# One fp32 transformer layer on one core: gate rows by two fp32r products, a reordered lead-in, and sixteen loads from GpSimd that nobody reads

## The chip, the core and the metric

The kernel runs on one NeuronCore of a Trainium2 chip. The core has five engines with an in-order instruction queue each: TensorE (PE, matrix products into PSUM), VectorE (DVE), ScalarE (ACT), GpSimd (POOL) and SyncE (SP, which here only issues transfers). Sixteen DMA engines move data between HBM and the on-chip memory (SBUF). The metric is the device time of one execution in microseconds, lower is better.

## The reference

The layer takes 256 latent tokens and 256 context tokens of width 2048, with fp32 weights:

```
sh1, sc1, g1, sh2, sc2, g2 = split(silu(c) @ w_ada + b_ada, 6)          # c is one row; 2048 -> 6 x 2048
x = layer_norm(alpha * x + g1 * (attention(x, ctx) @ w_out), ln1)       # modulated inputs, w_in, 16 heads
u = x * (1 + sc2) + sh2
x = layer_norm(alpha * x + g2 * ((silu(u @ w_gate) * (u @ w_up)) @ w_down), ln2)
```

`w_gate` and `w_up` are 2048 x 5632, `w_down` is 5632 x 2048. Only `g2`, the gate of the last residual, matters to the arithmetic of the change: it is a row of 2048 numbers, needed on all 128 partitions.

## The kernel before, in words

**Products.** Each fp32 weight piece is split into a high and a low part in fp32r: ACT copies the raw piece to `hi` (a cast), DVE subtracts (`lo = raw - hi`), and three PE products hi x hi, lo x hi and hi x lo replace one fp32 product (`mm3`, L292 to L294). Raw pieces of 1 MB (four tiles of 128 x 512) land in a ring of four buffers `raw`; split halves (128 x 1024) live in a ring of four slots `hi`/`lo`. A raw buffer is free for the next load when DVE has made its second `lo`.

**The lead-in** (first 25 us). A planner (`Flow`) orders the steps of the whole first phase with estimated times; some steps are then "pulled" to a place by hand (`F.pulls`: a trigger step, and the steps emitted right behind it). At the start two 1 MB pieces of `w_ada` come in four quarters each, PE multiplies them by silu(c) as they land (`flow_columns`, function `quarters`, L595), and the result modulates the first 128 columns of x and ctx: an ACT step and a DVE step `modulate`, then the low part `rest`. The first piece of `w_in` is split meanwhile (steps `w0`, `l0`: cast and low part), then pieces 1, 2 and 3 (`lead["w", i]`). Fillers (`warm`, L342) are small products of a constant, issued in gaps of PE. `evacs` are the copies of finished sums out of PSUM: rows 0 and 2 on ACT (L778), rows 1 and 3 on DVE (L782).

**The last stage** (from about 878 us). `w_down` is applied in four column blocks of 512 (n = 0 to 3), each in eleven steps of four tiles (`step`, 24 PE products for the 256 tokens), which I call steps 0 to 10. Beside it the gate row `g2` is made, 512 columns at a time (`gate2_steps`): GpSimd clears `adav` (L393), SP loads 512 numbers of `b_ada` into its first partition (L399), four loads of 1 MB of `w_ada` follow (L406), and DVE accumulates each of their sixteen tiles, scaled by silu(c), into `adav` (L416). One PE product with a 128 x 128 matrix of ones in plain fp32 (`rows_from`, L426) sums over the partitions and puts the row on all of them, and ACT copies it to `g2sb` (L427). There are four such rows; rows 0 and 1 are made during n = 0, rows 2 and 3 during n = 1 and n = 2. There is one buffer `adav`, so GpSimd may clear it for the next row only when the last row's product has read it.

In this stage the tile framework decides the order on each engine from simulated times; SP issues `w_down`, `w_ada` and `b_ada` loads from one queue, in that order, and a load that waits for its buffer or its semaphore holds all loads behind it.

Of the kernel before, what the change touches and what calls it, by code (L numbers as in the profile page):

```python
# [12 lines left out]
F32 = mybir.dt.float32  # L13
F32R = mybir.dt.float32r
# [4 lines left out]
ALU = mybir.AluOpType  # L19
# [3 lines left out]
P = 128  # L23
D = 2048
# [11 lines left out]
NB = 512  # L36
G4 = 4
SUB = 2
# [179 lines left out]
def dit_layer(ctx: ExitStack, tc: tile.TileContext, x, c, cx, c_ctx, w_ada, b_ada, w_in, q_norm_g,  # L218
              k_norm_g, sink_logit, w_out, ln1_g, ln1_b, w_gate, w_up, w_down, ln2_g, ln2_b,
              rope_cos, rope_sin, out):  # L220
    nc = tc.nc
    x, c, cx = x[0], c, cx[0]
    w_ada, w_in, w_out, w_gate, w_up, w_down = (w[0] for w in (w_ada, w_in, w_out, w_gate, w_up, w_down))
# [3 lines left out]
    whl = ctx.enter_context(tc.tile_pool(name="whl", bufs=HL_BUFS))  # L227
# [3 lines left out]
    def acc_bank():  # L231
        return acc_ps.tile([P, NB], F32, tag="acc", name="acc")

    def wk_bank():
        return wk_ps.tile([P, NB], F32, tag="wk", name="wk")

    def run(steps):
        for s in steps:
            s()

    def merge(*lists):

        keyed = [((i + 0.5) / len(l), n, i, s) for n, l in enumerate(lists) for i, s in enumerate(l)]
        return [e[3] for e in sorted(keyed, key=lambda e: e[:3])]
# [42 lines left out]
    def split(hi, lo, src):  # L287
        nc.scalar.copy(hi, src)
        nc.vector.tensor_tensor(lo, src, hi.bitcast(F32), op=ALU.subtract)
# [50 lines left out]
    def warm(wps, n):  # L340
        for _ in range(n):
            nc.tensor.matmul(wps, lhsT=ident, rhs=ident, start=True, stop=True)  # L342

    wps = Buf("wk")
# [16 lines left out]
    ones = main.tile([P, P], F32, tag="ones", name="ones")  # L361
# [10 lines left out]
    def ada_vector_steps(starts, width, sums, done):  # L372


        st = {}
        ns = len(starts)
        w = ns * width
        nk = G4 * NB // w

        def step(g):  # L380
            if g == 0:
                st["a"] = first_sums(sums(), starts, width)
            raw = raw_tile()
            vector_load(raw, starts, width, g)
            for i in range(G4 * NB // min(w, 2 * NB)):
                vector_sum(raw, st["a"], w, g, i)
            if g == KD // nk - 1:
                done(st["a"])

        return [lambda g=g: step(g) for g in range(KD // nk)]  # L390
# [29 lines left out]
    def vector_sums(width):  # L420
        return main.tile([P, 2 * NB], F32, tag="adav", name="adav")[:, :width]

    def rows_from(sb, dst, s):

        ps = wk_bank()
        nc.tensor.matmul(ps, lhsT=ones, rhs=sb[:, s : s + NB], start=True, stop=True)  # L426
        return lambda: nc.scalar.copy(dst[:, s : s + NB], ps)  # L427

    def ada_rows(c0, dst, sums):
        def done(sb):  # L430
            for s in range(0, dst.shape[-1], NB):
                rows_from(sb, dst, s)()

        return ada_vector_steps((c0,), dst.shape[-1], sums, done)

# [24 lines left out]
    def const_tables():  # L460
        nc.gpsimd.tensor_scalar_mul(nsink, sinkb, -1.0)
        for t in range(NT):
            for g, cg, sg in ((gq, cosQ, sinQ), (gk, cosK, sinK)):
# [18 lines left out]
    F = Flow({"raw": RAW_BUFS, "araw": ADA_BUFS, "hl": HL_BUFS, "acc": 4, "wk": 4, "b4": NB4, "t2k": T2K},  # L482
             {"SP": 2100.0, "PE": 3800.0, "ACT": 4300.0, "DVE": 4000.0, "POOL": 4000.0})
# [6 lines left out]
    def t2k(name, shape=(P, NB), dtype=F32):  # L490
        return pa.tile(list(shape), dtype, tag="t2k", name=name, bufs=T2K)
# [87 lines left out]
    last_load, lead = [], {}  # L579

    def flow_columns(c0, ncol, shift, scale, ats, at):

        width = ncol * P
        n1 = ncol == 1
        nk = G4 * NB // width
        ns = KD // nk
        bank, prev = Buf("wk"), None

        def fn(g, i, raw, k0, k1):
            if g == i == k0 == 0:  # L590
                bank.t = wk_bank()
            for c in range(k0, k1):
                k = g * nk + c
                j = k % 4
                nc.tensor.matmul(  # L595
                    bank.t[32 * j : 32 * j + 32, :width], lhsT=cs[:, 4 * k + 2 - 2 * i : 4 * k + 34 - 2 * i],
                    rhs=raw.t[:, c * width : (c + 1) * width],
                    start=(i == 0 and k < 4), stop=(i == 1 and k >= KD - 4),
                )

        for g in range(ns):
            F.at = ats[g]
            (r0, l0), (r1, l1) = (flow_load(w_ada, g * nk, nk, c0 + i * D, width, cut=1 if c0 else 4) for i in range(2))
            last_load[:] = [l1]
            ns1 = nk / 4 * (40 + 1.67 * width)
            if c0:
                def both(g=g, r0=r0, r1=r1):
                    fn(g, 0, r0, 0, nk)
                    fn(g, 1, r1, 0, nk)

                prev = F.add("PE", 2 * ns1 + 420, both, [l0, l1, prev], [bank] if g == 0 else [], [r0, r1])
            else:
                def quarters(i, r):
                    for q in range(4):
                        fn(0, i, r, 4 * q, 4 * q + 4)
                        if i and 0 < q < 3:
                            warm(wps.t, 1)

                prev = F.add("PE", ns1, lambda r=r0: quarters(0, r), [l0, prev], [bank] if g == 0 else [], [r0])
                lead["sum"] = prev  # L620
                prev = F.add("PE", ns1, lambda r=r1: quarters(1, r), [l1, prev], [], [r1])
            if g == 0:
                lead[c0, "both"] = prev
        F.at = at
        sb, ps = Buf("t2k"), Buf("wk")

        def copy():
            sb.t = t2k("ada")
            nc.scalar.copy(sb.t[:, :width], bank.t[:, :width])

        def sums():
            ps.t = wk_bank()
            for j in range(ncol):
                nc.tensor.matmul(ps.t[:, 4 * j : 4 * j + 4], lhsT=sb.t[:, j * P : (j + 1) * P], rhs=sel, start=True, stop=True)

        def add(i):
            pv = ps.t[:, 0 : 4 * ncol].rearrange("p (j i s) -> p j i s", i=2, s=2)
            bs, bc = (bcol[:, k : k + ncol, None].to_broadcast([P, ncol, 2]) for k in (c0 // P, c0 // P + KD))
            if i == 0:
                nc.vector.tensor_tensor(shift, pv[:, :, 0, :], bs, op=ALU.add)  # L640
            else:
                nc.vector.scalar_tensor_tensor(scale, pv[:, :, 1, :], 1.0, bc, op0=ALU.add, op1=ALU.add)

        a = F.add("ACT", 60 + 0.9 * width, copy, [prev], [sb], [bank])
        b = F.add("PE", 224 * ncol, sums, [a], [ps], [sb])
        adds = [F.add("DVE", 160, lambda i=i: add(i), [b], give=[ps]) for i in range(2)]
        if n1:
            lead[c0, "copy"], lead[c0, "sums"], lead[c0, "adds"] = a, b, adds
        return a, adds
# [91 lines left out]
    evacs = {}  # L741
# [364 lines left out]
    def second_modulation(g, sums):  # L1106
        def done(sb):
            ps = folded_columns(sb, 8)
            ks = slice(g * 4, g * 4 + 4)
            nc.vector.tensor_copy(sh2[:, ks, 0], ps[:, 0:4])  # L1110
            nc.vector.tensor_scalar_add(sc2[:, ks, 0], ps[:, 4:8], 1.0)
            combine(g)

        return ada_vector_steps((3 * D + g * NB, 4 * D + g * NB), NB, sums, done)
# [133 lines left out]
    start = F.add("SP", 0, lambda: None, at=1e5)  # L1248
# [3 lines left out]
    for g in range(last):  # L1252
        n = GROUPS[g][1]
# [153 lines left out]
    (flip0, mod0, rest0), (flip1, mod1, rest1) = (lead[0, s] for s in range(2))  # L1407
    (w0, l0), (w1, l1) = (lead["w", i] for i in range(2))
    F.pulls.append((lead["sum"], [flip0, flip1]))
    F.pulls.append((lead[0, "adds"][1], [w0, mod0, l0, rest0, mod1, rest1, w1, l1]))  # L1410
    for i in (2, 3):
        F.pulls.append((lead["evacs"][2 * i - 3], list(lead["w", i])))
    (flip0, mod0, rest0), (flip1, mod1, rest1) = (lead[P, s] for s in range(2))
    made = lead["products", 0]
    F.pulls.append(((lead["products", 1], 3), [lead[2 * P, "both"]]))
# [12 lines left out]
    pb = ctx.enter_context(tc.tile_pool(name="pb", bufs=1, reuse_waits="tile"))  # L1428
    u2h = pb.tile([P, KD, SEQ], F32R, tag="u2h", name="u2h")
# [119 lines left out]
    side = sum((second_modulation(g, late_sums[g - EARLY_G]) for g in range(EARLY_G, ng)), [])  # L1549
# [77 lines left out]

    l2 = pb.tile([P, 2, D], F32, tag="u2l", name="l2")
    l2g, l2b = l2[:, 0, :], l2[:, 1, :]
    g2sb = pb.tile([P, D], F32, tag="u2h", name="g2sb")  # L1630

    def l2_loads():
        nc.sync.dma_start(l2g, ln2_g[0:1, :].to_broadcast([P, D]))
# [2 lines left out]
    def gate2_steps(n):  # L1636
        return ada_rows(5 * D + n * NB, g2sb[:, n * NB : (n + 1) * NB], lambda: vector_sums(NB))
# [94 lines left out]
    for n in range(4):  # L1732
        steps = down_steps(n, [acc_bank() for _ in range(NT)]) if n < 3 else last_steps()
        side = (gate2_steps(0) if n == 0 else []) + (gate2_steps(n + 1) if n < 3 else [l2_loads])
        run(merge(steps, side))


# [46 lines left out]
```

## Time and profile before

| | |
|---|---|
| median of 3 runs | 1136.79 us (1134.44 to 1137.56) |
| profiled execution: its time / its span | 1134.76 us / 1133.0 us |
| granted TensorE clock, mean | 0.997 |
| PE busy | 1111.8 us (98% of the span) |
| DVE / ACT / POOL busy | 841.2 / 547.5 / 39.7 us |
| HBM traffic | 304.07 MB read, 16.25 MB written |

The prediction quotes rows of the profile. In a row of the timeline stand start, duration, engine (a trailing q is the queue that issues), source line, operation, out<-in, count, and in brackets the idle time before it with what ended it. A product's modelled duration (0.39 us) is longer than its pitch; the pitch is the difference of the starts. In a row of the windows stand the stretch, its length, the busy time of PE, PEld, DVE, ACT and POOL with instruction counts, the granted clock, the mean share of the DMA engines and GB/s. In a row of the waits stand who waited for whom, us in total, times, and the longest in us.

### The profile page before, as it was taken

What the parts mean: (1) busy time and instruction counts of PE and PEld (TensorE: products, weight loads), DVE (VectorE), ACT (ScalarE), POOL (GpSimd) and SP (SyncE); (2) the same over time, 40 slices, a digit from 0 to 9 for tenths busy, and PEclk for the clock granted to TensorE, in tenths of its full rate; (3) what the DMA queues carried; (4) which work ended last, traced back from release to release, by engine and by line L of the source; (5) the groups of instructions that cost most, each with busy time, mean ns of one, the idle gap of its engine ahead of it and who ended that gap; (6) DMA issues with size and microseconds to landing.
All of it is one profiled execution on the core that took longest, in us unless ns stands there. A gap on an engine that the chain in (4) does not pass through costs nothing.

```text
span 1133.0 us, 14075 instructions
## 1 busy us (share of the span) xinstructions
PE 1111.8 (98%) x5259; PEld 892.6 (79%) x5259; DVE 841.2 (74%) x1066; ACT 547.5 (48%) x790; POOL 39.7 (4%) x82
## 2 busy tenths in 40 slices
PE   8999999999999999999999999999999999999996
PEld 6666588788887787888888888888888888888884
DVE  4763589999989987877767566767766787676576
ACT  3341464877774365454464444445444344333342
POOL 1000050110100001000000000000000000000000
PEclk9999999999999999999999999999999999999998
DMA  9999999686999689998866766777677889877641
GB/s 306 365 393 396 386 370 370 238 261 200 372 334 391 230 309 343 320 326 307 312 223 217 251 223 224 243 243 255 217 249 243 311 314 328 318 283 245 203 147 74
DMA packets 178317, 321.26 MB, mean 284 GB/s; under 512 B 8732, under 2 KB 43196, under 8 KB 175943
## 3 DMA queue, kind: packets, MB, share of 16 engines
q1 hardware_dynamic: 177528, 320.03, 80.9%
q8 instruction: 41, 0.67, 0.2%
q10 hardware_dynamic: 720, 0.33, 0.1%
q14 instruction: 28, 0.23, 0.1%
HBM read 304.07 MB, written 16.25 MB: 283 GB/s over the span
## 4 chain that ended last, share of the span: by engine, by line
PE 91%; DMA 4%; DVE 2%; ACT 2%; issue 0%; POOL 0%; DVEq 0%; SPq 0%; ACTq 0%; POOLq 0%
PE acc L292 28%; PE acc L294 27%; PE acc L293 27%; PE wk L1025 2%; PE wk L595 2%; DMA raw<-in_w_in_dram 2%; DMA raw<-in_w_ada_dram 1%; DMA pd<-hx 1%; DVE lo L546 1%; PE wk L292 1%; PE wk L294 1%; PE wk L293 1%; DMA raw<-in_w_gate_dram 1%; DVE lo L283 1%; ACT hi L543 0%
## 5 line engine op out<-in xcount | busy, mean ns | idle before, releaser
L283 DVE TENSOR_TENSOR lo<-raw,hi 128x1024 fp32r<-128x1024 f32 x258 | 311.8, 1221 | 173.2 <-ACT hi L282 170.4
L282 ACT CAST hi<-raw 128x1024 fp32r<-128x1024 f32 x258 | 270.6, 1055 | 334.7 <-PE acc L294 296.5
L292 PE MATMUL acc<-hi,u2h 128*128 128x512 f32 x704 | 274.7, 390 | 0.2 <-ACT hi L282 0.2
L293 PE MATMUL acc<-lo,u2h 128*128 128x512 f32 x704 | 274.1, 389 | 0.8 <-DVE lo L283 0.8
L294 PE MATMUL acc<-hi,u2l 128*128 128x512 f32 x704 | 274.0, 389 | 0.0
L293 PEld LDWEIGHTS acc<-lo,u2h 128*128 128x128 f32 x704 | 132.2, 188 | 28.5 <-DVE lo L283 1.1
L292 PEld LDWEIGHTS acc<-hi,u2h 128*128 128x128 f32 x704 | 132.1, 188 | 28.5 <-ACT u2h L1559 0.8
L294 PEld LDWEIGHTS acc<-hi,u2l 128*128 128x128 f32 x704 | 132.1, 188 | 27.9 <-DVE u2l L1560 0.5
L543 ACT CAST hi<-raw 128x1024 fp32r<-128x1024 f32 (+1 forms) x86 | 87.7, 1030 | 107.4 <-DMA raw<-in_w_in_dram 51.3
L292 PE MATMUL acc<-hi,hTh 128*128 128x512 f32 x344 | 135.6, 394 | 0.4 <-ACT acc L1709 0.4
L294 PE MATMUL acc<-hi,hTl 128*128 128x512 f32 x344 | 133.9, 389 | 0.0
L293 PE MATMUL acc<-lo,hTh 128*128 128x512 f32 x344 | 133.9, 389 | 0.0
L416 DVE SCALAR_TENSOR_TENSOR adav<-raw,cs,adav 128x512 f32<-128x512 f32 (+1 forms) x128 | 121.3, 948 | 12.3 <-DMA raw<-in_w_ada_dram 10.3
L546 DVE TENSOR_TENSOR lo<-raw,hi 128x1024 fp32r<-128x1024 f32 (+1 forms) x86 | 101.7, 1193 | 17.3 <-ACT hi L543 17.3
L292 PE MATMUL acc<-hi,uh 128*128 128x512 f32 x256 | 103.1, 403 | 2.6 <-DVE kvacc L782 1.1
L293 PE MATMUL acc<-lo,uh 128*128 128x512 f32 x256 | 100.3, 392 | 2.0 <-DVE lo L546 2.0
L294 PE MATMUL acc<-hi,ul 128*128 128x512 f32 x256 | 100.2, 392 | 0.3 <-DVE ul L727 0.3
L292 PEld LDWEIGHTS acc<-hi,hTh 128*128 128x128 f32 x344 | 64.6, 188 | 15.2 <-issue 1.0
L293 PEld LDWEIGHTS acc<-lo,hTh 128*128 128x128 f32 x344 | 64.6, 188 | 14.3 <-issue 0.7
L294 PEld LDWEIGHTS acc<-hi,hTl 128*128 128x128 f32 x344 | 64.6, 188 | 13.3
L292 PEld LDWEIGHTS acc<-hi,uh 128*128 128x128 f32 x256 | 48.1, 188 | 20.4 <-issue 7.0
L293 PEld LDWEIGHTS acc<-lo,uh 128*128 128x128 f32 x256 | 48.1, 188 | 12.0 <-DVE lo L546 3.0
(219 smaller groups left out, 1137.6 us busy)
## 6 DMA issues: line engine op xcount, KB each, us to landing
raw<-in_w_ada_dram SPq DMA_DIRECT2D x70, 1024.0 KB, 7.0
raw<-in_w_gate_dram SPq DMA_DIRECT2D x44, 1024.0 KB, 5.2
raw<-in_w_up_dram SPq DMA_DIRECT2D x44, 1024.0 KB, 5.1
raw<-in_w_down_dram SPq DMA_DIRECT2D x44, 1024.0 KB, 4.9
raw<-in_w_ada_dram SPq DMA_DIRECT2D x48, 512.0 KB, 5.2
raw<-in_w_in_dram SPq DMA_DIRECT2D x18, 1024.0 KB, 7.0
raw<-in_w_out_dram SPq DMA_DIRECT2D x16, 1024.0 KB, 8.0
pd<-hx SPq DMA_DIRECT2D x64, 128.0 KB, 4.1
```

Of the source, the lines that this page charges most:

```text
L282: nc.scalar.copy(hi[:, :n], raw[:, s : s + n])
L283: nc.vector.tensor_tensor(lo[:, :n], raw[:, s : s + n], hi[:, :n].bitcast(F32), op=ALU.subtract)
L292: nc.tensor.matmul(ps, lhsT=xh, rhs=w[0], start=first, stop=False, skip_group_check=seeded)
L293: nc.tensor.matmul(ps, lhsT=xh, rhs=w[1], start=False, stop=False, skip_group_check=seeded)
L294: nc.tensor.matmul(ps, lhsT=xl, rhs=w[0], start=False, stop=last, skip_group_check=seeded)
L416: nc.vector.scalar_tensor_tensor(a[:, c : c + piece], raw[:, f : f + piece], cs[:, 4 * (g * (G4 * NB // w) + j) + 2, None], a[:, c : c + p ...
L543: nc.scalar.copy(hl.hi[:, :n], raw.t[:, s : s + n])
L546: nc.vector.tensor_tensor(hl.lo[:, :n], raw.t[:, s : s + n], hl.hi[:, :n].bitcast(F32), op=ALU.subtract)
L595: nc.tensor.matmul(bank.t[32 * j : 32 * j + 32, :width], lhsT=cs[:, 4 * k + 2 - 2 * i : 4 * k + 34 - 2 * i], rhs=raw.t[:, c * width : (c + ...
L1025: nc.tensor.matmul(o_ps.t[:, : 2 * P].rearrange("p (g q) -> p g q", q=32), lhsT=v, rhs=pv[:, k], start=k == 0, stop=k == 3)
```

## The change

1. Gate rows: `split_rows` takes the place of `rows_from` for the four rows of `g2`. The sum `adav` is split into `hi` (ACT) and `lo` (DVE) in a slot of the ring of four, and two fp32r products with a ones matrix in fp32r (`onesr`, made once by ACT) take the place of one fp32 product.
2. Lead-in: no fillers between the quarters of the second `w_ada` piece; the low part `l0` of the first `w_in` piece is emitted before the first modulation instead of after it; casts and low parts of pieces 2 and 3 are each pulled by one evacuation, one or two evacuations sooner.
3. `g2sb` gets a second half (the tile is as large as the `u2h` whose room it takes). GpSimd clears that half and then issues sixteen loads of 512 KB each of `w_down` data into its two quarters in turn: eight that add to what is there, eight that convert fp32 to fp32r. Nothing reads them.

```diff
+    def split_rows(sb, dst, s):
+        hi = whl.tile([P, SUB * NB], F32R, tag="hi", name="hi")[:, :NB]
+        lo = whl.tile([P, SUB * NB], F32R, tag="lo", name="lo")[:, :NB]
+        split(hi, lo, sb[:, s : s + NB])
+        ps = wk_bank()
+        nc.tensor.matmul(ps, lhsT=onesr, rhs=hi, start=True, stop=False)
+        nc.tensor.matmul(ps, lhsT=onesr, rhs=lo, start=False, stop=True)
+        nc.scalar.copy(dst[:, s : s + NB], ps)
...
-                rows_from(sb, dst, s)()
+                split_rows(sb, dst, s)
...
                 def quarters(i, r):
-                    for q in range(4):
-                        fn(0, i, r, 4 * q, 4 * q + 4)
-                        if i and 0 < q < 3:
-                            warm(wps.t, 1)
+                    fn(0, i, r, 0, nk)
...
-    F.pulls.append((lead[0, "adds"][1], [w0, mod0, l0, rest0, mod1, rest1, w1, l1]))
+    F.pulls.append((lead[0, "adds"][1], [w0, l0, mod0, rest0, mod1, rest1, w1, l1]))
     for i in (2, 3):
-        F.pulls.append((lead["evacs"][2 * i - 3], list(lead["w", i])))
+        for j in range(2):
+            F.pulls.append((lead["evacs"][2 * i - 4 + j], [lead["w", i][j]]))
...
-    g2sb = pb.tile([P, D], F32, tag="u2h", name="g2sb")
+    g2all = pb.tile([P, 2 * D], F32, tag="u2h", name="g2sb")
+    g2sb = g2all[:, :D]
+    onesr = pb.tile([P, P], F32R, tag="onesr", name="onesr")
+    nc.scalar.copy(onesr, ones)
+    room = [g2all[:, D : D + 2 * NB], g2all[:, D + 2 * NB : 2 * D]]
+
+    def extra_load(i, cast):
+        if i == 0 and not cast:
+            nc.gpsimd.memset(g2all[:, D:], 0.0)
+        dst = room[i % 2].rearrange("p (k n) -> p k n", k=2)
+        src = w_down[i * 2 * P : (i + 1) * 2 * P, :NB].rearrange("(k p) n -> p k n", p=P)
+        if cast:
+            nc.gpsimd.dma_start(dst.bitcast(F32R), src)
+        else:
+            nc.gpsimd.dma_start(dst, src, accum_op=ALU.add)
...
+        if n in (1, 2):
+            side += [lambda n=n: [extra_load(i, n == 2) for i in range(8)]]
         run(merge(steps, side))
```

The built programs show where these instructions stand.

GpSimd's queue in the last stage, before: the last step of the first phase, and the clears of `adav` for gate rows 1, 2 and 3 (the brackets name the semaphores each waits for).

```order
L1073 TENSOR_TENSOR mB_150<-mB_150,sh2_147 128x4 [waits Pool_49]
L393 MEMSET adav_7663 128x512 [waits DMAHW3_49,DVE_49,PE_49]
L393 MEMSET adav_7917 128x512 [waits DMAHW6_49,PE_49]
L393 MEMSET adav_8331 128x512 [waits DMAHW1_49,DVE_49,PE_49]
L1779 UNCONDITIONAL_BRANCH
```

GpSimd's queue at the same place in the changed program, from the clear of the new half to the clear for row 1 (`adav_7668`); L1651 adds, L1649 converts, and DMASW are the semaphores of GpSimd's own transfers.

```order
L1645 MEMSET g2sb_7408 128x2048 [waits DMAHW1_49,DMAHW0_49,DMAHW7_49,DVE_49,PE_49]
L1651 DMA g2sb_7408<-in_w_down_dram 128x2x512 [waits Pool_49]
L1651 DMA g2sb_7408<-in_w_down_dram 128x2x512
L1651 DMA g2sb_7408<-in_w_down_dram 128x2x512 [waits DMASW0_49]
...
L1651 DMA g2sb_7408<-in_w_down_dram 128x2x512 [waits DMASW5_49]
L1649 DMA g2sb_7408<-in_w_down_dram 128x2x512 [waits DMASW6_49]
L1649 DMA g2sb_7408<-in_w_down_dram 128x2x512 [waits DMASW7_49]
L1649 DMA g2sb_7408<-in_w_down_dram 128x2x512 [waits DMASW0_49]
L1649 DMA g2sb_7408<-in_w_down_dram 128x2x512 [waits DMASW1_49]
L393 MEMSET adav_7668 128x512 [waits DMAHW3_49,DVE_49]
```

All eight adding loads and four of the converting ones now stand ahead of the clear for row 1, each waits for the transfer two before it, and that clear no longer waits for PE.

SP's queue around the `b_ada` load of row 1 (`adav`, L399), before: `raw_7672` and `raw_7706` are the pieces of `w_down` for steps 6 and 7 of n = 0, `raw_7750` for step 8.

```order
L406 DMA raw_7666<-in_w_ada_dram 128x4x512 [waits DMAHW3_49,DVE_49]
L262 DMA raw_7672<-in_w_down_dram 128x4x512 [waits DMAHW4_49,DVE_49]
L262 DMA raw_7706<-in_w_down_dram 128x4x512 [waits DMAHW5_49,DVE_49]
L399 DMA adav_7663<-in_b_ada_dram 1x512 [waits DMAHW6_49,Pool_49]
L1493 DMA hf_7740<-hd_7653 128x512 [waits DMAHW7_49]
L1493 DMA hf_7742<-hd_7658 128x512 [waits DMAHW2_49,DMAHW1_49,DMAHW0_49]
L406 DMA raw_7744<-in_w_ada_dram 128x4x512 [waits DVE_49]
L262 DMA raw_7750<-in_w_down_dram 128x4x512 [waits DMAHW4_49,DVE_49]
```

The same place in SP's queue of the changed program, where `raw_7677` and `raw_7711` are the pieces for steps 6 and 7.

```order
L406 DMA raw_7671<-in_w_ada_dram 128x4x512 [waits DMAHW3_49,DVE_49]
L399 DMA adav_7668<-in_b_ada_dram 1x512 [waits DMAHW4_49,Pool_49]
L262 DMA raw_7677<-in_w_down_dram 128x4x512 [waits DMAHW5_49]
L262 DMA raw_7711<-in_w_down_dram 128x4x512 [waits DMAHW6_49]
L1500 DMA hf_7745<-hd_7658 128x512 [waits DMAHW7_49]
L1500 DMA hf_7747<-hd_7663 128x512 [waits DMAHW2_49,DMAHW1_49,DMAHW0_49]
L406 DMA raw_7749<-in_w_ada_dram 128x4x512 [waits DVE_49]
L262 DMA raw_7755<-in_w_down_dram 128x4x512 [waits DMAHW3_49,DVE_49]
```

The `b_ada` load, which waits for GpSimd's clear, moved ahead of the pieces for steps 6 and 7.

VectorE's queue in the lead-in, before (from the modulation of x to the first evacuations of the query sums):

```order
L712 TENSOR_SCALAR uf_234<-wk_184,scc_120,shc_119 128x256
L546 TENSOR_TENSOR lo_232<-raw1_193,hi_231 128x512
L727 TENSOR_TENSOR ul_236<-uf_234,uh_235 128x256
L712 TENSOR_SCALAR uf_241<-wk_187,scc_120,shc_119 128x256
L727 TENSOR_TENSOR ul_243<-uf_241,uh_242 128x256
```

VectorE's queue at that place in the changed program:

```order
L555 TENSOR_TENSOR lo_230<-raw1_193,hi_229 128x512
L718 TENSOR_SCALAR uf_233<-wk_184,scc_120,shc_119 128x256
L733 TENSOR_TENSOR ul_235<-uf_233,uh_234 128x256
L718 TENSOR_SCALAR uf_239<-wk_187,scc_120,shc_119 128x256
L733 TENSOR_TENSOR ul_241<-uf_239,uh_240 128x256
```

The low part of the first `w_in` piece went ahead of the modulation; on ACT the cast of piece 2 went, in the same way, from behind the second evacuation to between the two.

## The prediction

> **What bounds the kernel now.** I read the page first: its totals and the chain that ended last.
>
> ```profile
> span 1133.0 us, 14075 instructions
> PE 1111.8 (98%) x5259; PEld 892.6 (79%) x5259; DVE 841.2 (74%) x1066; ACT 547.5 (48%) x790; POOL 39.7 (4%) x82
> PE 91%; DMA 4%; DVE 2%; ACT 2%; issue 0%; POOL 0%; DVEq 0%; SPq 0%; ACTq 0%; POOLq 0%
> ```
>
> PE is the bound: nine tenths of the chain are PE's own work. So PE time that goes is time gained, and a wait put on PE is time lost; work elsewhere counts only when it makes PE wait. In the last stage the thing that could do so is supply, so I went to the waits of SP's queue, and then to the timeline where the largest of the clears' waits lies.
>
> ```profile
> SPq L399 <- POOL adav L393: 26.3, 4, 9.0
> 892.20 0.39 SPq L406 DMA_DIRECT2D raw<-in_w_ada_dram  x1
> 895.38 2.64 SPq L262 DMA_DIRECT2D raw<-in_w_down_dram  x2
> 906.57 0.53 POOL L393 MEMSET adav<- 128x512 f32 x1 [339.21 <-PE wk L426]
> 907.12 0.26 SPq L399 DMA_DIRECT2D adav<-in_b_ada_dram  x1
> 907.43 0.82 SPq L1493 DMA_DIRECT2D hf<-hd  x2
> 909.36 0.38 SPq L262 DMA_DIRECT2D raw<-in_w_down_dram  x1
> ```
>
> SP stood 9.0 us, to 907.12, at the `b_ada` load of gate row 1, because GpSimd could clear `adav` only when PE had used row 0. The two `w_down` pieces of 895.38 (steps 6 and 7) had gone out ahead. The piece for step 8 went at 909.36, and what became of it is in ACT's and DVE's timeline:
>
> ```profile
> 892.23 3.12 DVE L416 SCALAR_TENSOR_TENSOR adav<-raw,cs,adav 128x512 f32<-128x512 f32 x4 [0.56 <-DMA raw<-in_w_ada_dram]
> 898.87 1.05 ACT L282 CAST hi<-raw 128x1024 fp32r<-128x1024 f32 x1 [3.02 <-PE acc L294]
> 918.29 2.00 ACT L282 CAST hi<-raw 128x1024 fp32r<-128x1024 f32 x2 [4.60 <-DMA raw<-in_w_down_dram]
> 925.47 2.00 ACT L282 CAST hi<-raw 128x1024 fp32r<-128x1024 f32 x2 [5.17 <-DMA raw<-in_w_down_dram]
> 926.56 2.36 DVE L283 TENSOR_TENSOR lo<-raw,hi 128x1024 fp32r<-128x1024 f32 x2 [0.54 <-ACT hi L282]
> ```
>
> Normally the cast waits for PE (898.87: a slot of the ring comes free). At 918.29 and 925.47 it waits for the transfer instead. PE did not wait yet, but the reserve is thin. PE's rows give the schedule:
>
> ```profile
> 878.27 0.39 PE L292 MATMUL acc<-hi,hTh 128*128 128x512 f32 x1
> 905.25 0.40 PE L294 MATMUL acc<-hi,hTl 128*128 128x512 f32 x1
> 905.48 1.02 PE L426 MATMUL wk<-adav,ones 128*128 128x512 f32 x2
> 906.58 0.39 PE L293 MATMUL acc<-lo,hTh 128*128 128x512 f32 x1
> ```
>
> The stage begins at 878.27 and row 0's product starts after five steps at 905.48: (905.48 - 878.27) / 5 = 5.44 us a step, 0.227 us a product. The row costs 906.58 - 905.25 less two pitches, 1.33 - 0.45 = 0.88 us. So step 6 begins at 905.48 + 0.88 + 5.44 = 911.80, and step 9 three steps later, at 928.1; its first `lo`, half of 926.56's 2.36 us, is ready at 927.8 and wanted one product after the start, at 928.3. The reserve is 0.5 us.
>
> **The change part by part.** *Gate rows.* Four plain fp32 products of 0.88 us become four pairs at two pitches, 0.45 us: 4 x 0.43 = 1.7 us gained, all on PE's path. The added cast and subtraction (ACT and DVE, half the size of 898.87's and 926.56's, some 1.3 us a row) lie beside PE. Row 0's sums end at 892.23 + 3.12 = 895.4, its product stands at 905.5: hidden by 10 us. They also take one of four slots of the ring for half a step; if that cover went, a step would start up to one cast later, 1 us a row. I take nothing.
>
> *Lead-in.* Rows of the timeline, the fillers first:
>
> ```profile
> 10.40 0.16 PEld L595 LDWEIGHTS wk<-raw,cs 128*32 128x32 f32 x8 [0.16 <-DMA raw<-in_w_ada_dram]
> 10.76 0.49 PE L342 MATMUL wk<-ident 128*128 128x128 f32 x2
> 11.18 0.42 PE L595 MATMUL wk<-raw,cs 128*32 128x128 f32 x8
> 11.84 0.62 ACT L543 CAST hi<-raw 128x512 fp32r<-128x512 f32 x1
> 13.28 0.54 DVE L712 TENSOR_SCALAR uf<-wk,scc,shc 128x256 f32<-128x256 f32 x1 [0.64 <-ACT uh L710]
> 13.73 0.68 DVE L546 TENSOR_TENSOR lo<-raw,hi 128x512 fp32r<-128x512 f32 x1
> 14.47 0.51 PE L293 MATMUL acc<-lo,uh 128*128 128x512 f32 x1 [0.67 <-DVE lo L546]
> 18.29 1.23 DVE L546 TENSOR_TENSOR lo<-raw,hi 128x1024 fp32r<-128x1024 f32 x1 [0.89 <-ACT hi L543]
> 19.43 0.68 DVE L782 COPY kvacc<-acc 128x512 f32<-128x512 f32 x1
> 20.18 0.50 PE L292 MATMUL acc<-hi,uh 128*128 128x512 f32 x1 [0.77 <-DVE kvacc L782]
> 20.00:25.00 5.00, 4.50 (x18) 3.22 (x18) 4.30 (x8) 1.17 (x2) 0.00 (x0) 1.00 1.06 338
> ```
>
> Quarter 3 waited for its data until 10.40, so the filler ahead of it was free. Quarter 4 started at 11.18, 0.8 us later, about what 256 KB take at 338 GB/s (estimate from the last row), so that filler hid a transfer too: 0 us, at most the 0.4 of 10.76. The low part is worth more. Its `hi` is done at 12.46 and DVE is idle 0.64 us before 13.28; with `lo` at 12.64 the modulation ends 0.4 us sooner and PE's third product with it. Later DVE idles 0.89 us before 18.29 for a cast that ACT made behind two evacuations. With the cast between them the copy of 19.43, which holds PE for 0.77 us at 20.18, is done before PE asks. Together 1.1 us. Late next are DVE's copies of the query sums. Above it is bounded by those two waits, 1.2 us; below by 0, since the DMA engines are full (share 1.06) and PE may only arrive earlier at a later transfer. I take 1.1: PE frees the buffers that trigger the transfers behind.
>
> *The sixteen loads.* GpSimd clears the new half as soon as PE is done with `u2h`, at 878.3, then issues twelve loads before it may clear `adav` for row 1. Each waits for the one two before it, so there are two in flight, and the clear comes after ten landings: four rounds of adding loads and one of converting ones. Queued behind that clear are, on SP, row 1's `b_ada` load and the pieces for steps 6 and 7. No transfer of GpSimd is in this trace. The nearest rows:
>
> ```profile
> 1.35 1.80 POOL L1121 MEMSET g1b<- 128x2048 f32 x1
> raw<-in_w_ada_dram SPq DMA_DIRECT2D x70, 1024.0 KB, 7.0
> raw<-in_w_down_dram SPq DMA_DIRECT2D x44, 1024.0 KB, 4.9
> raw<-in_w_ada_dram SPq DMA_DIRECT2D x48, 512.0 KB, 5.2
> raw<-in_w_out_dram SPq DMA_DIRECT2D x16, 1024.0 KB, 8.0
> pd<-hx SPq DMA_DIRECT2D x64, 128.0 KB, 4.1
> 880.00:890.00 10.00, 10.00 (x46) 8.28 (x45) 8.37 (x11) 3.83 (x5) 0.00 (x0) 1.00 0.94 296
> 890.00:900.00 10.00, 10.00 (x45) 8.28 (x45) 6.85 (x9) 3.58 (x4) 0.00 (x0) 1.00 1.05 375
> 900.00:910.00 10.00, 10.00 (x43) 7.89 (x42) 5.53 (x5) 3.64 (x4) 0.53 (x1) 1.00 0.51 188
> ```
>
> A converting load is 512 KB: 5.2 us. An adding load reads 512 KB and also what it adds to, so I price it as 1024 KB beside other traffic: 7.0 us. The clear for row 1 then comes at 878.3 + 1.8 + 4 x 7.0 + 5.2 = 913.3, instead of 906.57.
>
> When must it come? From clear to `b_ada` load 907.12 - 906.57 = 0.55, then 0.31 to SP's next issue, 4.9 us landing, cast 1.05, first `lo` 1.2, less one product: 7.8 us. Step 6 begins, with the shorter row, at 911.4; so the limit is 903.6, and PE waits 913.3 - 903.6 = 9.7 us. The lead-in moves both sides alike. Nothing gives this back, because PE has no slack later. Bounds on a round: 4.1 us (the 128 KB row, the shortest landing of its kind) gives 878.3 + 1.8 + 5 x 4.1 = 900.6, before the limit, no wait. Twice the 8.0 of `w_out` for an adding load (two at once in full engines) gives 880.1 + 64 + 8 = 952, a wait of 48 us. I take the middle rows because the engines are nearly full at 880 to 900 (shares 0.94 and 1.05) but half free from 900 on, where SP stands. The last four converting loads fall into the thin stretch after 913; I count nothing for them, at most one landing, 5 us.
>
> [...]
>
> *Sum:* -1.7 - 1.1 + 9.7 = +6.9 us on the profiled execution's 1134.8 (span 1133.0 and 1.8 around it), 1141.7. The median of the runs shown, 1136.8, lies 2.0 above that execution, so the forecast is 1143.7.
>
> **The rivals.**
> *No wait (the other side).* A round under (903.6 - 880.1) / 5 = 4.7 us keeps the clear ahead of the limit. It may even come before 906.57, since it waits no more for PE, and SP's 9.0 us shrink. For it: the half-empty stretch 900 to 910. Against: 5.2 us for 512 KB from SP, without adding. Time: 1136.8 - 2.8 = 1134.0, a little lower if the lead-in gives more.
> *The loads crowd out SP's own.* In 880 to 900 the engines are full, so each load of GpSimd delays row 0's last `w_ada` piece, for which DVE waited 0.56 us already and behind which it holds step 4's `lo`; rounds of 12 us put the clear at 880.1 + 48 + 8 = 936, a wait of 32.5 us: 1166. For it: share 1.05. Against: SP stops at 893 and leaves the engines to GpSimd.
> *Rows late.* The split's slot or DVE's wait for ACT delays each row by up to 1 us: without a wait for supply 1134.0 + 4 = 1138. Against: 10 us between row 0's sums and its product.
>
> **How the numbers follow.** My forecast has 0.45, no wait 0.30, crowding 0.20, rows late 0.05. A difference below 0.3%, 3.4 us, can't be told from no change: below 1133.4 is faster, above 1140.2 slower. Of the 0.30 I put 0.10 below 1133.4 (the lead-in giving 0.6 us more than its rows show) and 0.20 within; rows late is within; of the forecast's 0.45 0.03 have waits under 6.2 us. So faster 0.10, same 0.28, slower 0.62. The range goes from 1133 (no wait) to 1166 (crowding).
>
> **What would show it.** Right: POOL's clear of `adav` for row 1 ends near 913 and SP's `b_ada` load waits for it; PE has one gap of some 10 us near 911 that ends with a `lo` or `hi` of `w_down`; GpSimd's adding loads take some 7 us a pair; the four rows take 0.45 us each; PE is 1.1 us earlier at 25 us. Wrong: no PE gap in the last stage; a gap with the clear early (then crowding, not the queue); PE gaps in the first 90 us that eat the lead-in.

## The result, and the profile after

| | before | after |
|---|---|---|
| median | 1135.9 us (4 runs, 1134.4 to 1137.6) | 1179.9 us (4 runs, 1178.1 to 1182.1) |
| profiled execution: time / span | 1134.8 / 1133.0 us | 1181.4 / 1179.6 us |
| mean granted TensorE clock | 0.997 | 0.978 |

The change makes the kernel slower: the ratio is 1.039, 95% interval 1.036 to 1.042, or 44 us. I had forecast 1143.7 and a range up to 1166. The place was right, the size was not.

The totals of the page of the changed kernel, its clock in forty slices, its GpSimd queue and its chain:

```profile
PE 1113.8 (94%) x5255; PEld 894.3 (76%) x5255; DVE 845.3 (72%) x1070; ACT 549.1 (47%) x795; POOL 56.8 (5%) x99
PEclk9999999999999999999999999999999589999998
q0 software_dynamic: 4352, 8.39, 3.4%
PE 80%; DMA 8%; issue 5%; DVE 4%; ACT 2%; POOL 1%; ACTq 0%; DVEq 0%; SPq 0%; POOLq 0%
```

PE is busy 2 us longer than before (1111.8 us then), so some 45 of the 47 us by which the span grew are idle time of PE. Nearly all of them lie in one place: the clock falls in slices 32 and 33, 914 to 973 us. The chain has 5% of "issue", time in which an engine waited for nothing that the profile shows. GpSimd's timeline there:

```profile
878.88 1.81 POOL L1645 MEMSET g2sb<- 128x2048 f32 x1 [310.92 <-PE acc L293]
881.03 1.40 POOL L1651 DMA_DIRECT2D g2sb<-in_w_down_dram  x1 [0.34 <-POOL g2sb L1645]
890.35 1.23 POOL L1651 DMA_DIRECT2D g2sb<-in_w_down_dram  x1 [7.92 <-issue]
899.64 1.19 POOL L1651 DMA_DIRECT2D g2sb<-in_w_down_dram  x1 [8.06 <-issue]
912.86 1.19 POOL L1651 DMA_DIRECT2D g2sb<-in_w_down_dram  x1 [4.96 <-issue]
932.25 1.21 POOL L1651 DMA_DIRECT2D g2sb<-in_w_down_dram  x1 [5.33 <-issue]
932.98 1.23 POOL L1649 DMA_DIRECT2D g2sb<-in_w_down_dram  x1
938.75 0.72 POOL L1649 DMA_DIRECT2D g2sb<-in_w_down_dram  x1 [4.54 <-DMA g2sb<-in_w_down_dram]
944.03 0.54 POOL L393 MEMSET adav<- 128x512 f32 x1
```

The eight adding loads (L1651) go out one at a time, 9.3 us apart at first, 7.1 once, and 6.2 to 6.5 us apart later. The second waits for no semaphore, yet stands 7.92 us on "issue". The converting loads (L1649) wait for a landing by name, as the semaphores say. The clear of `adav` for gate row 1 comes at 944.03; I had it at 913.3.

What stood behind it, in the timelines of SP, DVE and PE:

```profile
894.59 0.39 SPq L406 DMA_DIRECT2D raw<-in_w_ada_dram  x1
944.60 0.25 SPq L399 DMA_DIRECT2D adav<-in_b_ada_dram  x1
944.90 0.94 SPq L262 DMA_DIRECT2D raw<-in_w_down_dram  x2
947.20 1.54 DVE L416 SCALAR_TENSOR_TENSOR adav<-raw,cs,adav 128x512 f32<-128x512 f32 x2 [44.01 <-DMA adav<-in_b_ada_dram]
948.66 1.22 DVE L283 TENSOR_TENSOR lo<-raw,hi 128x1024 fp32r<-128x1024 f32 x1
907.89 0.39 PE L292 MATMUL acc<-hi,hTh 128*128 128x512 f32 x1
949.93 0.79 PE L293 MATMUL acc<-lo,hTh 128*128 128x512 f32 x1 [41.65 <-DVE lo L283]
950.52 0.63 PE L294 MATMUL acc<-hi,hTl 128*128 128x512 f32 x1
```

SP stands 50 us at the `b_ada` load. DVE stands too: the first sums of row 1 (L416) come in its order ahead of the second `lo` of step 5, whose data had long been there. So PE stops in step 5, 41.65 us long, and restarts at half speed. DVE is not what holds the loads up: it idles for 44 us, and they stand on "issue" all the same. The windows show the restart, and what the DMA engines did meanwhile:

```profile
915.00:920.00 5.00, 0.00 (x0) 0.00 (x0) 0.00 (x0) 0.00 (x0) 0.71 (x1) 0.50 0.62 101
920.00:925.00 5.00, 0.00 (x0) 0.00 (x0) 0.00 (x0) 0.00 (x0) 0.51 (x1) 0.50 0.71 105
950.00:955.00 5.00, 5.00 (x15) 3.97 (x16) 1.29 (x2) 0.24 (x1) 0.38 (x1) 0.64 1.07 329
955.00:960.00 5.00, 4.17 (x18) 2.90 (x17) 3.30 (x3) 3.77 (x5) 1.05 (x2) 1.00 1.10 394
```

At a granted clock of 0.50 products come every 0.43 us instead of 0.227 until 953.5; some eight of them cost 1.7 us. And the engines are busy 0.62 and 0.71 for 101 and 105 GB/s, while the kernel before needed 0.94 for 296, about half as much for a byte. These rows don't show that it is the adding, and not that these loads come alone or in other packets; two runs below do.

To keep the scatter of the 880 us ahead out of it, I compare profiles by the length of the last stage, from its first product to the end of the span: 254.7 us before (1133.0 less 878.27), 300.7 after (1179.6 less 878.88).

### The profile page after: what moved, and what is told of

The parts are those of the page before. It is cut to its first block, busy times and chain, and to the rows that moved or that the text cites. A ratio compares the mean times of both kernels' runs of the same rounds, so it can differ in the third digit from the quotient of the medians.

```text
span 1179.6 us, 14098 instructions
## 1 busy us (share of the span) xinstructions
PE 1113.8 (94%) x5255; PEld 894.3 (76%) x5255; DVE 845.3 (72%) x1070; ACT 549.1 (47%) x795; POOL 56.8 (5%) x99
## 3 DMA queue, kind: packets, MB, share of 16 engines
q0 software_dynamic: 4352, 8.39, 3.4%
## 4 chain that ended last, share of the span: by engine, by line
PE 80%; DMA 8%; issue 5%; DVE 4%; ACT 2%; POOL 1%; ACTq 0%; DVEq 0%; SPq 0%; POOLq 0%
PE acc L292 24%; PE acc L293 24%; PE acc L294 24%; PE wk L1031 2%; DMA raw<-in_w_ada_dram 2%; DMA raw<-in_w_in_dram 2%; PE wk L604 2%; DMA raw<-in_w_down_dram 1%; DVE lo L283 1%; POOL g2sb L1651 1%; DMA pd<-hx 1%; DVE adav L416 1%; DMA raw<-in_w_up_dram 1%; DVE lo L555 1%; PE wk L292 1%
## 5 line engine op out<-in xcount | busy, mean ns | idle before, releaser
L282 ACT CAST hi<-raw 128x1024 fp32r<-128x1024 f32 x258 | 270.0, 1053 | 366.0 <-PE acc L294 284.5
L416 DVE SCALAR_TENSOR_TENSOR adav<-raw,cs,adav 128x512 f32<-128x512 f32 (+1 forms) x128 | 121.3, 948 | 58.9 <-DMA adav<-in_b_ada_dram 44.0
L294 PEld LDWEIGHTS acc<-hi,u2l 128*128 128x128 f32 x704 | 132.2, 188 | 28.5 <-DVE u2l L1567 1.1
L292 PEld LDWEIGHTS acc<-hi,u2h 128*128 128x128 f32 x704 | 132.2, 188 | 28.5 <-ACT u2h L1566 0.8
L294 PEld LDWEIGHTS acc<-hi,ul 128*128 128x128 f32 x256 | 48.1, 188 | 12.0 <-DVE ul L733 1.9
```

The source lines that it names most:

```text
L282: nc.scalar.copy(hi[:, :n], raw[:, s : s + n])
L292: nc.tensor.matmul(ps, lhsT=xh, rhs=w[0], start=first, stop=False, skip_group_check=seeded)
L294: nc.tensor.matmul(ps, lhsT=xl, rhs=w[0], start=False, stop=last, skip_group_check=seeded)
L416: nc.vector.scalar_tensor_tensor(a[:, c : c + piece], raw[:, f : f + piece], cs[:, 4 * (g * (G4 * NB // w) + j) + 2, None], a[:, c : c + p ...
```

## The experiments

**What the loads cost as a whole.** Theory: they are all of the loss, and the gate rows and the lead-in gain what they were priced at. The rival: the split rows themselves hold up DVE or SP. First the change without its loads.

```diff
-        if n in (1, 2):
-            side += [lambda n=n: [extra_load(i, n == 2) for i in range(8)]]
```

> The change without its sixteen loads: the gate rows from split sums and the new lead-in alone. Theory (the loads are the whole loss): no gap in the last stage, time = 1135.9 - 1.7 (gate rows) - 0 to 1.1 (lead-in) = 1133.1 to 1134.2; the clear of adav for row 1 now waits only for DVE's split and comes near 897. Rival (the split rows themselves hold the order of DVE or SP): a gap in the last stage stays, time over 1150.

1132.5 us, ratio 0.997 (0.9954 to 0.9986), 0.6 us under the expected range: the loads cost 47 us, and the rest of the change is a gain of 0.3%. PE waits 0.4 us in the whole last stage, as before, so the rival is out. The clear for row 1, from GpSimd's timeline:

```profile
899.73 0.53 POOL L393 MEMSET adav<- 128x512 f32 x1 [332.97 <-DVE lo L289]
```

It comes 7 us earlier than before, since the split has read `adav` long before PE multiplies. The last stage takes 253.0 us, 1.7 less than before.

The two parts of that gain, each alone: the gate rows without loads and with the old lead-in,

```diff
-                    fn(0, i, r, 0, nk)
+                    for q in range(4):
+                        fn(0, i, r, 4 * q, 4 * q + 4)
+                        if i and 0 < q < 3:
+                            warm(wps.t, 1)
...
-    F.pulls.append((lead[0, "adds"][1], [w0, l0, mod0, rest0, mod1, rest1, w1, l1]))
+    F.pulls.append((lead[0, "adds"][1], [w0, mod0, l0, rest0, mod1, rest1, w1, l1]))
...
-        for j in range(2):
-            F.pulls.append((lead["evacs"][2 * i - 4 + j], [lead["w", i][j]]))
+        F.pulls.append((lead["evacs"][2 * i - 3], list(lead["w", i])))
```

> The kernel before with the gate rows from split sums only. Theory: 4 x 0.43 us on PE's path, 1135.9 - 1.7 = 1134.2. If the lead-in's gain lasts to the end, the kernel with both parts and no loads is 1.1 us below this one; if it is lost to full DMA engines after 25 us, the two are equal within 0.3 us. Rival (rows late): over 1136.

and the new lead-in without loads and with the old rows.

```diff
-                split_rows(sb, dst, s)
+                rows_from(sb, dst, s)()
```

> The kernel before with the new lead-in only. Theory (the gain of 1.1 us at 25 us lasts to the end): 1136.0 - 1.1 = 1134.9, the two parts adding up to the 1132.5 of both within the noise. Rival (lost to full DMA engines between 25 and 150 us): 1136.0, no change.

The rows alone: 1133.9 us, ratio 0.9985 (0.997 to 1.0), a last stage of 253.0 us. The lead-in alone: 1132.8 us, ratio 0.9985 (0.9972 to 0.9998). Each ratio is 1.7 us, with intervals that just reach or just leave out no change, and together they make the 3.4 us of the first run. The rows' part shows in the stage's length. The lead-in alone leaves that length at 254.6 us, so its part must lie ahead, and there the profiles can't settle it: in the thirteen with the new lead-in the stage starts anywhere from 875.8 to 880.9 us, in the two without at 878.3 and 878.8. That the lead-in's gain reaches the end is likely from the medians, not shown beyond doubt.

**Queue or traffic.** Theory: the loads hurt by standing ahead of the clear on GpSimd. Rival: their traffic keeps SP's transfers out. So the four clears of the last stage go to DVE, and all loads stay; SP's order is that of the change.

```diff
-        nc.gpsimd.memset(a, 0.0)
+        (nc.vector if starts[0] >= 5 * D else nc.gpsimd).memset(a, 0.0)
```

> The whole change, but the four clears of adav in the last stage are made by VectorE instead of GpSimd; all sixteen loads stay, and so does SP's order. Theory (GpSimd's own order: the clear stands behind twelve loads): the gap near 908 to 950 is gone, time 1134 to 1140, with some slower landings of w_down beside the loads. Rival (the loads' traffic keeps SP's transfers out): the gap stays, PE waits over 20 us in the last stage, time over 1155.

1144.0 us, ratio 1.0065 (1.0047 to 1.0084): the gap is gone and 36 us with it, but 8.3 us above before are left, more than the theory allowed. PE's waits in the last stage, and DVE's from 870 to 1000 us:

```profile
PE acc L293 <- DVE lo L283: 5.6, 6, 2.0
PE acc L292 <- ACT hi L282: 2.4, 3, 1.1
DVE adav L416 <- DMA raw<-in_w_ada_dram: 16.9, 6, 5.8
```

Nine waits of at most 2 us each: DVE waits for `w_ada` pieces that land late, and PE for the low parts behind. That looks like traffic, but DVE's clears could be at fault, so here they are without loads.

```diff
-        nc.gpsimd.memset(a, 0.0)
+        (nc.vector if starts[0] >= 5 * D else nc.gpsimd).memset(a, 0.0)
...
-        if n in (1, 2):
-            side += [lambda n=n: [extra_load(i, n == 2) for i in range(8)]]
```

> VectorE makes the four clears and there are no extra loads: what the clears on VectorE cost by themselves, with the same kernel with loads at 1144.0 and the one with neither at 1132.5. Theory (the 11.6 us between those are the loads' traffic): 1131 to 1134, and no wait of PE in the last stage. Rival (VectorE's order pays for the clears): 1138 to 1144.

1131.9 us, ratio 0.9967 (0.9952 to 0.9983): the clears cost nothing on DVE, and the traffic of sixteen loads costs 12 us (1144.0 - 1131.9). So the theory holds for the gap, and the rival as it was put, a gap that stays and over 1155 us, fell; what is left of it are the 12 us. 36 us are GpSimd's order and 12 are traffic, though the change, in whose gap SP sends nothing, need not pay both in full.

**Adding or converting.** The converting loads alone:

```diff
-        if n in (1, 2):
+        if n == 2:
             side += [lambda n=n: [extra_load(i, n == 2) for i in range(8)]]
```

> The change with the eight converting loads only; they stand ahead of the clear for row 1. Theory (plain and converting loads run two in flight, 8 us a pair beside SP's traffic as the plain ones did): 877 + 30 = 907 for the clear, within 4 us of what PE can bear, and some traffic: 1134 to 1142. Rival (converting loads are as slow as the adding ones, 7 to 9 us each): clear near 940, time over 1165.

1141.2 us, ratio 1.0034 (1.0015 to 1.0052). All eight stand ahead of the clear, which comes 28.6 us after the first of them was issued; in GpSimd's, PE's and the windows' rows:

```profile
880.22 1.67 POOL L1649 DMA_DIRECT2D g2sb<-in_w_down_dram  x2 [311.19 <-PE acc L294]
908.77 0.55 POOL L393 MEMSET adav<- 128x512 f32 x1
914.96 0.80 PE L293 MATMUL acc<-lo,hTh 128*128 128x512 f32 x1 [5.23 <-DVE lo L283]
915.00:920.00 5.00, 5.00 (x12) 3.94 (x13) 3.66 (x4) 1.99 (x2) 0.00 (x0) 0.50 1.05 401
```

Here is a wait of the kind that I had forecast, 5.2 us where I had 9.7, with the converting loads alone. It costs 8.7 us of the last stage (261.7 against 253.0): 5.2 are the wait, and 2.8 come because the clock stays at 0.50 for six more microseconds (14 products at 0.43 us). With the eight adding loads turned into plain ones:

```diff
-            nc.gpsimd.dma_start(dst, src, accum_op=ALU.add)
+            nc.gpsimd.dma_start(dst, src)
```

> The whole change, but the eight adding loads only write (same bytes, same rooms, same order on GpSimd). Theory (an adding load waits until the one ahead has landed, which a plain load does not): two in flight, about 2.6 us each as the converting loads have it, eight in 21 us; the clear for row 1 comes near 880.7 + 21 + 11 = 913, some 31 us sooner than 944, time 1147 to 1152. Rival (any GpSimd load of this size runs one at a time, 6.2 us or more each): the clear stays near 944, time 1178 to 1182.

1152.8 us, ratio 1.0144 (1.0125 to 1.0163), 0.8 us over the expected range, with all five engines in the order of the change. GpSimd:

```profile
879.04 1.68 POOL L1651 DMA_DIRECT2D g2sb<-in_w_down_dram  x2 [0.33 <-POOL g2sb L1645]
887.32 0.72 POOL L1651 DMA_DIRECT2D g2sb<-in_w_down_dram  x1 [6.60 <-DMA g2sb<-in_w_down_dram]
907.52 0.72 POOL L1649 DMA_DIRECT2D g2sb<-in_w_down_dram  x1 [1.85 <-DMA g2sb<-in_w_down_dram]
916.38 0.54 POOL L393 MEMSET adav<- 128x512 f32 x1
```

Two are in flight, eight take 28.5 us instead of 51.95 (932.98 - 881.03), the clear comes 37.3 us after the first load instead of 63.0 (944.03 - 881.03), and the time is 27 us less. So the price of adding is over half of the loss. But why one at a time?

**What holds an adding load back.** My first theory was that such a load waits until everything ahead of it has landed. I let the two kinds alternate (GpSimd still clears the new half once, ahead of them), and halved the size in another kernel.

```diff
-            side += [lambda n=n: [extra_load(i, n == 2) for i in range(8)]]
+            side += [lambda n=n: [extra_load(i, i % 2 == 0) for i in range(8)]]
```

> The sixteen loads with converting and adding ones in turn, a converting one first; each room then takes only one kind. Theory (an adding load is issued only when every earlier load of GpSimd has landed, of whatever kind): the first adding load, which waits on no semaphore for a load, idles 5 to 9 us behind the first converting one, while a converting load follows an adding one at once. Rival (an adding load waits only for an earlier adding load): the first adding load follows within 2 us, and the idle time before adding loads begins with the second one.

```diff
-            nc.gpsimd.dma_start(dst, src, accum_op=ALU.add)
+            nc.gpsimd.dma_start(dst[:, :1], src[:, :1], accum_op=ALU.add)
```

> The change with adding loads of half the size, 256 KB each; the clear for row 1 now stands behind all eight and six converting loads. Theory (an adding load costs its landing, which shrinks with the bytes): 4 to 5 us from one to the next where SP stands still, against 6.3; the clear 55 us after the stage's start, time 1166 to 1174. Rival (a fixed price for each adding load): 6.2 us or more each, clear 68 us after, time 1180 to 1186.

The first adding load after a converting one (L1654 after L1652), and the first of the half size, which count as two in one row:

```profile
880.40 0.95 POOL L1652 DMA_DIRECT2D g2sb<-in_w_down_dram  x1 [0.33 <-POOL g2sb L1648]
881.35 1.27 POOL L1654 DMA_DIRECT2D g2sb<-in_w_down_dram  x1
889.18 0.74 POOL L1652 DMA_DIRECT2D g2sb<-in_w_down_dram  x1 [6.55 <-DMA g2sb<-in_w_down_dram]
878.43 1.99 POOL L1651 DMA_DIRECT2D g2sb<-in_w_down_dram  x2 [0.33 <-POOL g2sb L1645]
886.48 0.84 POOL L1651 DMA_DIRECT2D g2sb<-in_w_down_dram  x1 [6.07 <-DMA g2sb<-in_w_down_dram]
```

The theory of the first run fell: the adding load follows the converting one at once, and none of the eight stands on "issue". Its rival, that an adding load waits only for an earlier adding one, could not show there, because each load waits by semaphore for the one two before it, which is the last of its kind. It fell in the second run, with both theories of that run: two adding loads of half the size are in flight together, at a pitch between pairs (8.1 us) like that of plain loads. The times were 1165.8 and 1154.7 us, one run each. In the half-size program SP has one `w_down` piece ahead of row 1's `b_ada` load, so its time stands apart. What is left is room: two small ones fit, a large and a converting one fit, two large ones don't. The program sets one size for GpSimd's loads, `dynamic_dma_scratch_size=1024`, which I call the room. So: the change with more room, 1536 bytes (the edit shown) and 2048 (with 192 bytes less of padding in the main pool), and plain loads with less, 512, where by the count of the first expectation no two would go together.

```diff
-    nc = _bacc.Bacc("TRN2", target_bir_lowering=False, num_devices=1, dynamic_dma_scratch_size=1024)
+    nc = _bacc.Bacc("TRN2", target_bir_lowering=False, num_devices=1, dynamic_dma_scratch_size=1536)
```

> [...] Theory (the room holds three of: an adding load of 512 KB counts two, a converting one, a plain one or an adding one of 256 KB counts one, so two adding loads don't fit in 1024 but do in 1536): the second adding load is issued within 2 us of the first and the later ones wait for a landing by semaphore; the clear for row 1 comes 40 to 50 us after the stage's start instead of 65, time 1153 to 1165. Rival (adding loads of 512 KB go one at a time whatever the room): nothing changes, clear at 65, 1178 to 1182.

> The same with 2048 bytes (and 192 bytes less of padding in the main pool). [...] Rival (whatever the room): 1178 to 1182. If 1536 changes nothing and this does, the room is right and the count of units is wrong.

> The change with plain loads in place of the adding ones (1152.8 with 1024 bytes of room), now with 512 bytes. [...] Rival (only adding loads are held up): clear 39 after, 1151 to 1155.

GpSimd's first loads with 1536 bytes and its clear, then plain ones with 512 bytes:

```profile
878.47 2.64 POOL L1651 DMA_DIRECT2D g2sb<-in_w_down_dram  x2 [0.34 <-POOL g2sb L1645]
888.38 1.21 POOL L1651 DMA_DIRECT2D g2sb<-in_w_down_dram  x1 [7.27 <-DMA g2sb<-in_w_down_dram]
924.13 0.54 POOL L393 MEMSET adav<- 128x512 f32 x1
877.97 0.94 POOL L1651 DMA_DIRECT2D g2sb<-in_w_down_dram  x1 [0.31 <-POOL g2sb L1645]
885.84 0.74 POOL L1651 DMA_DIRECT2D g2sb<-in_w_down_dram  x1 [6.93 <-issue]
936.75 0.54 POOL L393 MEMSET adav<- 128x512 f32 x1
```

With 1536 bytes two adding loads go out together, "issue" is gone, and the time is 1163.4 us, ratio 1.0262 (1.0241 to 1.0284), 16 us less with every engine's order unchanged; 2048 bytes gave 1166.2 in one run, 1.2 over the range expected with 1536, with two in flight as well. With 512 bytes plain loads stand on "issue" as the adding ones did: 1171.9 us in one run, 19 more than with 1024. The room is the cause, both ways.

How much does an adding load take? The 4352 packets on the page of the change are 17 for each of 16 loads on each of 16 DMA engines: 16 rows of 2 KB and one more. The queue's row with the converting loads alone, then with plain ones in place of the adding ones, and a stretch of the run with 512 bytes, in which SP rests and one converting load is in flight at a time:

```profile
q0 software_dynamic: 2176, 4.19, 1.2%
q0 software_dynamic: 3328, 8.39, 2.2%
925.00:930.00 5.00, 0.00 (x0) 0.00 (x0) 0.00 (x0) 0.00 (x0) 0.72 (x1) 0.50 0.51 137
```

Eight converting loads keep the sixteen engines busy for 1.2% of 1141.7 us, 13.7 us. In the change, 3.4% of 1179.6 us less these leave 26 us for the eight adding ones, about twice as much with as many packets, and plain ones take 12. A converting load that comes alone, too, needs only 0.51 for 137 GB/s. So it is the adding that doubles the engine time.

By these runs two adding loads need more than 1024 bytes and at most 1536. That 64 more would do was a guess of mine, from a count that no run shows. So the whole change with 1088 bytes, where I expected two in flight and 1160 to 1167 us:

```diff
+    nc = _bacc.Bacc("TRN2", target_bir_lowering=False, num_devices=1, dynamic_dma_scratch_size=1088)
```

> [...] 512 bytes let no two plain loads stand together, 1024 let two plain or an adding and a converting one but not two adding ones, 1536 let two adding ones. [...] Theory B (the room is shared in whole loads or by bytes, and two adding loads need well more than 1024): still one at a time, clear 65 after, 1178 to 1182.

```profile
883.00 2.64 POOL L1651 DMA_DIRECT2D g2sb<-in_w_down_dram  x2 [0.34 <-POOL g2sb L1645]
892.47 1.20 POOL L1651 DMA_DIRECT2D g2sb<-in_w_down_dram  x1 [6.82 <-DMA g2sb<-in_w_down_dram]
928.80 0.54 POOL L393 MEMSET adav<- 128x512 f32 x1
```

1167.4 us, ratio 1.0279 (1.026 to 1.0298): two in flight, and the clear 45.8 us after the first load, as with 1536 bytes (45.7) and not as in the change (63.0). The limit lies between 1024 and 1088 bytes; what fills the room is not shown by that. Packets alone don't: an adding load has as many as a converting one (17 an engine), and in 1024 bytes one of each goes together, as at 932.25 and 932.98 in the change, but two adding ones don't. The time is 0.4 us over the expected range and 4 us over that of 1536 bytes, with intervals that overlap; in the length of the last stage, which leaves out the scatter ahead, the two are 284.5 and 282.8 us.

## Why the prediction was right and wrong

**Gate rows: right.** The pair took the two pitches foreseen, at 906.08 and 906.31 with the next product at 906.53 in PE's timeline, and 1.7 us came out, in the stage's length and in the rows alone. The rival "rows late" did not come.

**Lead-in: right, a little small.** The fillers were free: without them PE still waited 0.38 and 0.33 us for the quarters. The rows of the changed kernel, PE's first, with the copy whose wait was to go and the block of 64 `w_ada` products that follows:

```profile
11.25 0.43 PE L604 MATMUL wk<-raw,cs 128*32 128x128 f32 x8 [0.33 <-DMA raw<-in_w_ada_dram]
12.63 0.68 DVE L555 TENSOR_TENSOR lo<-raw,hi 128x512 fp32r<-128x512 f32 x1
19.98 0.50 PE L292 MATMUL acc<-hi,uh 128*128 128x512 f32 x1 [0.23 <-DVE qacc L788]
23.61 1.95 PE L604 MATMUL wk<-raw,cs 128*32 128x128 f32 x64
```

The low part starts at 12.63 (I said 12.64), the wait for `kvacc` is gone, and DVE's copies of the query sums are late next, as said. (By the diff only the casts of pieces 2 and 3 go sooner, by one evacuation each; the low parts keep their trigger, though the list of changes says that both move.) The block of 64 starts at 23.61 against 25.08: 1.47 us, where I had taken 1.1 and bounded it at 1.2.

**The loads: the chain of waits was right, the price of a round was wrong.** The clear does hold SP's `b_ada` load and the pieces for steps 6 and 7. The limit was near: moved by the 0.6 us by which the stage starts later here, it is 904.2 for the clear's start (the sum counts from there, though the list of signs has 913.3 as the clear's end); the clear started at 944.03, so the wait should be 39.8, and it was 41.65. It fell in step 5 and not in step 6, because I had put only SP behind the clear and not DVE, whose sums stand in its own order. On that path the product at 949.93 comes 5.9 us after the clear's start and was wanted at 908.1, a limit of 902.2, which accounts for the other 2 us.

The step that failed is "there are two in flight", at 7.0 us a round. I read the semaphores in the order of instructions, and they allow two; the trace of before, with no load of GpSimd, could not show that the room doesn't. From the stage's start to the clear I had 35.0 us, and 65.15 came. The 30.15 between are, by the runs:

| | forecast | measured | |
|---|---|---|---|
| eight adding loads, if two are in flight | 28.0 | 36.9 (room of 1536) | +8.9 |
| the same, one at a time | - | 51.95 | +15.05 |
| converting loads ahead of the clear | 5.2 | 11.05 | +5.85 |
| clear of the new half, to the first issue | 1.8 | 2.15 | +0.35 |

My 7.0 us, the landing of one megabyte from SP beside other traffic, was what a pair of plain loads takes (28.5 for eight); a pair of adding ones took 9.2 where the room let them. I had counted one load's landing for a round of two, so the price was too low even with two in flight. That an adding load costs as much as two of its size was an assumption of mine. The engine time bears it out, 26 us for eight adding loads and 12 for eight plain ones; the landings do so less: one at a time, the eight plain ones of the 512-byte run took 3.8 us at the least and 4.1 in the median, the eight adding ones of the change 5.8 and 6.2.

**The bounds and the rivals.** A round of 16 us stood as the upper bound, with a wait of 48. The loads did run near 13 us a pair, but I gave that case no chance of its own and let the range end at crowding, with rounds of 12, at 1166. "No wait" was 46 us off. Crowding exists as a mechanism of its own, 12 us when nothing else stops; in the change, SP stood still for most of the loads, as I had held against it. "Nothing gives this back" held: past the gap come 2.7 us of smaller waits and the 1.7 of the slow clock.

The parts worth keeping are the rows and the lead-in: 1132.5 us, or 1131.9 with the clears on DVE.

## What to carry to other kernels

Before a load is issued from an engine, look at what stands behind it in that engine's order, and at who waits for that: here a clear of half a microsecond carried SP, DVE and PE with it, 41.65 us long. In the change the semaphores let two loads be in flight, and the room no more than one adding load: "issue" ahead of a load, 7.92 us with no releaser, was the sign, and 64 bytes more took 12 us off. A wait can cost more than its length: with the converting loads alone 5.2 us became 8.7, because the granted clock fell to 0.50 and PE ran at half speed for six more.

## What the runs showed of the hardware

- Room: two adding loads of 512 KB don't go together in 1024 bytes and do in 1088, so one takes over 512 and at most 544, if room simply adds up. Two plain ones don't in 512 and do in 1024: over 256 and at most 512. Whether an adding load takes twice the room of a plain one these bounds leave open.
- Engine time: eight adding loads kept the sixteen engines busy for 26 us, eight converting ones in as many packets for 14 (from the queue's rows).
- An adding load keeps GpSimd 1.2 us at the issue, against 0.72 for a plain or converting one and 0.85 for an adding one of half the size.
- Beside SP's traffic, pairs of 256 KB adding loads and of 512 KB plain ones both came 8 us apart (8.05 and 8.28 from the first pair to the second), as the doubled engine time of an added byte would have it.
- In the change the granted clock fell to 0.50 some 4.4 us after the end of PE's last product (907.89 + 0.39; 0.65 from 912.5 to 913.0, 0.50 from there on), and with the converting loads alone 4.5 us after (909.34 + 0.39; 0.92 from 910 to 915). It came back 3.6 us behind PE's restart in the change, after 41.65 us of rest, and 6.1 us behind it with the converting loads alone, after 5.2: the longer return followed the shorter rest.
